# A two-layer decoder trunk on one core: retention steps, x's forms and three sets of weight sums put at other places

## The chip, the core and the metric

The kernel runs on one core of one Trainium2 chip. The core has five engines that run side by side, each through its own list of instructions in order: TensorE (PE: matmuls, with the weight loads shown apart as PEld), VectorE (DVE), ScalarE (ACT), GpSimd (POOL, hardly used here) and SyncE (SP, whose queue issues nearly all transfers). They wait for each other by semaphores. Matmul results land in PSUM banks, from which DVE and ACT fetch them; all other tiles lie in SBUF. The metric is the time on the device in microseconds (us), lower is better.

## What is computed

Two layers of a decoder over 512 tokens of width 1024, then a final RMS norm. All in float32. Cut to one layer:

```python
h = rmsnorm(x, g_mix)
z = h @ w_in
aq, ak, av, rq, rk, rv, rg, ga, gb = jnp.split(z, SPLIT_POINTS, axis=-1)
...
ya = sliding_window_sink_attention(aq, ak, av, sinks) @ w_a
...
r = chunkwise_retention(rq, rk, rv)
r = r * lax.rsqrt(jnp.mean(r * r, axis=-1, keepdims=True) + EPS)
r = r.reshape(B, S, RET_V) * jax.nn.silu(rg.astype(jnp.float32))
yb = r.astype(x.dtype) @ w_b
mixed = jax.nn.sigmoid(ga) * ya + jax.nn.sigmoid(gb) * yb
x = x + mixed @ w_out
h2 = rmsnorm(x, g_mlp)
x = x + jnp.square(jax.nn.relu(h2 @ w_up)) @ w_down
```

Attention has 8 query heads of 64 and 2 key heads, in a window of 128. Retention has 4 heads with keys of 128 and values of 256; with no chunks it is, per head, a product of scores, decayed by distance, with the values. The feed-forward width is 4096.

## The kernel before

**Precision.** Every factor is split in two parts, `hi` (rounded to the format that PE takes) and `lo` (the rest), and each product is three matmuls: hi·hi, hi·lo, lo·hi (`products`, lines 351 to 359). So a weight unit of 128 x 1024 is loaded as `raw` by SP, turned into `hi` by an ACT copy (L311) and into `lo` by a DVE subtraction (L312). Raw, hi and lo have three buffers each: unit i+3 is loaded when the low part of unit i has been made, and split when PE has gone through unit i.

**Activations are transposed**: 128 features by 512 tokens per tile. `chunk` (L400) computes 128 columns of a product: one unit, 24 matmuls into one bank of `ps_mm` (five banks), then `evacuate`. Ahead of each half of 12 matmuls it calls `advance(rate)`.

**Background work.** Attention and retention are Python generators in the list `background`. `advance(rate)` (L384) adds `rate` to a credit and, for each whole credit, runs the first generator up to its next `yield`, which writes that piece's instructions into the program at this place; `drain` (L396) runs what is left. Places in the program set the priorities; a planner orders each engine's list by them and by its own estimate of when the inputs are there, and hands out the buffers of the pools.

**Retention** (`retention`, L1190) does two heads: for each, scores for two blocks and then for the other two (`Head.scores`, with a decay table `dm` in a single buffer), then the two halves of the outputs (`Head.outputs`), the norm (`Head.norm`; the last head's by `inverse_rms`, L499, with a matmul with ones at L503 and a reciprocal at L505), and `finish`: two multiplications per half (L1184, L1185) and a split (L364, L365). At its end `sum_input` (L657) makes the forms of the pair's results. Its yields:

```python
for head in two:
    for js in ((0, 1), (2, 3)):
        head.scores(js)
        yield
...
while 4 * pair + 3 not in rg:
    yield
```

**Forms.** Several products are computed in a scheme with fewer multiplications (seven block products in place of eight): the moving factor comes as sums of blocks (`sum_input`: four DVE operations L667 to L671 and two splits of 128 x 1024) and the weights as sums of blocks. `narrow_pair` (L692) does this for w_b and w_out, `wide_pair` for w_up, and in the second layer `all_values` (L1033) for retention's values. Its seven `multiply` calls take two units and 24 matmuls each; between them ACT and DVE copy, add and split the banks: `eu` and `bu` are copies of 128 x 512 pairs. For it the second layer loads x once more from DRAM (`spill`), scales it (L1030) and makes forms of it: `raw_forms` (L1024), called for blocks 0 and 2.

**Weight sums made ahead.** For nine pairs of units of the second layer the sums of weight blocks are made in advance and parked in DRAM: `load_ahead` (L630) loads two units of 512 KB into two `big` tiles, `sum_ahead` (L634) makes four sums on DVE, behind the latest low part, and stores four parts (L266 to L271); `ahead` is both. The lists `PARKED` (w_b 0 and 2, w_out 6, w_up 4 and 6) and `AHEAD_VALUES` (four for the values) say which, `to_load` in which order. The first layer makes its own five sets (`PARKED`) during its mixing stage; its feed-forward makes the second layer's nine: the first three (w_out 6, w_up 4, w_up 6) at the w_down steps of the first quarter (`q == 0`), six in the last quarter.

**Order in the second layer** (`layer_body`): q, k, v of attention; attention in the background of gate_a's chunks, `qk(0)` and four rg chunks (their results in two `big` tiles `z`); then `raw_forms` 0, `qk(1)` (two chunks, retention's rk and rq of head 1), `raw_forms` 2; the product with w_a; `all_values`; then `qk(2)`, `qk(3)`, rg 4 to 7 and eight gate_b chunks (`put_aside`, L966 and L967, stored to `aside`) at 1.25 steps a half chunk, with both retention pairs in the background; `drain`; the products with w_b (L1352 on), which read retention's results and their forms; w_out; the feed-forward. The `big` pool has seven tiles of 128 x 1024, the pool of small ones (`temp`, 128 x 512) six, `ps_aux` three banks.

Of the kernel before, what the change touches and what calls it, by code (L numbers as in the profile page):

```python
# [13 lines left out]
AF = mybir.ActivationFunctionType  # L14
# [119 lines left out]
def decoder(ctx, tc, xT, x_first, w_in, w_a, w_b, w_out, w_up, w_down, tables, decay, band, triangles, g_last, out):  # L134
# [504 lines left out]
    def ahead():  # L639
        sum_ahead()  # L640
        load_ahead()

    def layer_body(layer):
# [389 lines left out]
        def all_values(form):  # L1033

            a, (e, b) = [bank(ps_aux, "rv") for _ in range(2)], [[bank(p, "rv") for p in (q, ps_mm)] for q in (ps_aux, ps_mm)]
            eu, bu = big("eu"), big("bu")

            def keep_values(pair, n, src):
                hi, lo = slots.one(), slots.one()
                split(view(hi), view(lo), src, rcol[:, n : n + 1])  # L1040
                rv[pair, n] = (hi, lo)

            def multiply(two, moving, start):
                for u in range(2):
                    hi, lo = unit("value", layer)
                    for i in range(2):
                        k, cols = 2 * u + i, slice(i * T, (i + 1) * T)
                        for j, ps in enumerate(two):
                            m = moving[k][:, :, j * P : (j + 1) * P]
                            pair = ((m[:, 0, :], m[:, 1, :]), (hi[:, cols], lo[:, cols]))  # L1050
                            products(ps, [pair], start and k == 0, k == 3, not start)

            def add_up(pair, two, kept):
                for j in range(2):
                    nc.vector.tensor_tensor(kept[:, j, :], two[j], kept[:, j, :], ALU.add)
                    keep_values(pair, 2 + j, kept[:, j, :])

            multiply(a, block(0, 0), True)
            for j in range(2):
                nc.scalar.activation(b[j], a[j], AF.Copy)  # L1060
            multiply(e, form(0), True)
            for j in range(2):
                nc.scalar.activation(eu[:, j, :], e[j], AF.Copy)
            multiply(b, form(1), False)
            for j in range(2):
                nc.scalar.activation(bu[:, j, :], b[j], AF.Copy)
            multiply(a, block(1, 0), False)
            for j in range(2):
                keep_values(0, j, a[j])
            multiply(b, form(2), False)  # L1070
            add_up(1, b, eu)
            multiply(e, block(1, 1), False)
            add_up(0, e, bu)
            multiply(b, form(3), False)
            for j in range(2):
                keep_values(1, j, b[j])

        rg, rg_next, rg_tiles = {}, {}, {}

# [144 lines left out]
        qk(0, PACE)  # L1224
        for i in range(4):
            chunk("w_in", layer, xs, put_rg(i), PACE)
        load_ahead()
        load_ahead()
        drain()
        rstd_columns()  # L1230
        with tc.issue_after(last_exp[0]):
# [5 lines left out]
        if last_layer:  # L1237
            homes_v = [forms_home() for _ in range(4)]
            by_form_v = [h[1] for h in homes_v]
            raw_forms(by_form_v, 0)  # L1240
            qk(1)
            raw_forms(by_form_v, 2)
        else:
            qk(1, between=ahead)
            values(0, ahead)
# [3 lines left out]
        for u in range(4):  # L1249
            hi, lo = unit("w_a", layer)  # L1250
            for j in range(2):
                c = 2 * u + j
                ps = bank(ps_mm, "mm")
                pairs = []
                for k in range(4):
                    cols = slice(k * 256 + j * P, k * 256 + (j + 1) * P)
                    pairs.append(((hi[:, cols], lo[:, cols]), aT[k]))
                products(ps, pairs, True, True)
                nc.vector.tensor_tensor(mixed[c], mixed[c], ps, ALU.mult)
            if u != 2:  # L1260
                ahead()
        for t in a_t:
            slots.give(*t[1])

        if last_layer:
            all_values(form_of(by_form_v))
            for t, _ in homes_v:
                slots.give(*t[1])
            background.append(retention(0))
            qk(2, 1.25)  # L1270
            qk(3, 1.25)
        else:
            background.append(retention(0))
            qk(2)
            qk(3)
            values(1)
            drain()
        background.append(retention(1))
        for i in range(4, 8):
            chunk("w_in", layer, xs, put_rg(i), 1.25)  # L1280
        gates, gate_tiles, fresh = [], [], []

        def put_aside(c):
# [7 lines left out]
            return put  # L1291

        for c in range(KD):
            chunk("w_in", layer, xs, put_aside(c), 1.25)
        drain()
        old_input()

# [250 lines left out]

        turning = []
        if not last_layer:  # L1550
            to_load.extend((layer + 1, *at) for at in (*PARKED[2:], *PARKED[:2], *AHEAD_VALUES))
        for what, q, i in mlp_sequence():
            if what == "first":
                late = group("w_up", layer, xs, [put_up] * 4, first_hooks())
            elif what == "pair":
                pair(q, i, late)
                if (q, i) == (3, 3):
                    old_input()
                    for t, _ in homes_x:
                        slots.give(*t[1])  # L1560
            elif what == "down":
                if (layer, q, i) == (DEPTH - 1, 2, 2):
                    turning = turns(0)
                two_chunks("w_down", layer, up[q], [put_down(2 * i), put_down(2 * i + 1)], turning)
                if i == 3:
                    slots.give(*up_slots[q])
                if not last_layer and q == 0:
                    sum_ahead()
                    if i < 3:
                        load_ahead()  # L1570
            elif layer == DEPTH - 1:
# [202 lines left out]
```

## Time and profile before

| | us |
|---|---|
| median of 3 runs | 1480.32 (1478.83 to 1480.66) |
| the profiled execution, its time | 1481.1 |
| the profiled execution, its span | 1479.2 |
| first layer: up to | about 765 |
| second layer: value product | about 898 to 938 |
| second layer: qk(2) to the last gate_b chunk | about 938 to 1046 |
| second layer: feed-forward from | about 1130 |

The profile is one execution on the chip. Its page shows busy time and count per engine; the other views cut the same record by stretches of time, by waits, by tiles, or list it in order of time. A line such as `L311 ACT ACTIVATE hi<-raw` is: line of the kernel, engine, operation, tile written and tiles read. In a timeline row the first two numbers are start and duration in us, the last entry in brackets the idle time of that engine before it and what ended it. An idle engine costs time only where PE ends up waiting for it. Matmuls are pipelined: a busy PE says that work is there, and the granted clock (1.00 is full) how fast it goes.

### The profile page before, as it was taken

The numbers are of one execution on the slowest core, as the hardware profiler recorded it, in microseconds if no ns is written. First come the engines' busy times: TensorE is split into PE (matmuls) and PEld (weight loads), VectorE is DVE, ScalarE is ACT, GpSimd is POOL, SyncE is SP. The second block draws the span as 40 slices with busy tenths as digits, with TensorE's granted clock in tenths as the row PEclk, the third lists the DMA queues.
The fourth block names the chain that finished last, engine by engine and source line by source line (L and its number), as shares of the span: only waits on it lengthen the run. The fifth ranks groups of instructions, "written<-read, shape, count | busy, mean of one in ns | idle before, by whom it ended". The sixth has DMA issues, their size and how long they took to land.

```text
span 1479.2 us, 20294 instructions
## 1 busy us (share of the span) xinstructions
PE 1461.5 (99%) x7410; PEld 1244.8 (84%) x7410; DVE 1187.6 (80%) x1950; ACT 831.4 (56%) x1330; POOL 3.7 (0%) x14
## 2 busy tenths in 40 slices
PE   9999999999999999999999999999799999999998
PEld 7888888888988888888888878888789888888887
DVE  7998778678988887776898886867889877877774
ACT  6657356654784445544455675666546844445444
POOL 0000000000000000000000000000000000000000
PEclk9999999999999999999999999999899999999999
DMA  6423843256445443334973235423464433332363
GB/s 226 134 88 108 275 161 105 93 185 210 124 128 188 164 136 100 100 100 163 324 254 113 86 129 160 139 86 124 133 212 122 130 101 99 114 115 91 111 199 112
DMA packets 80547, 212.29 MB, mean 144 GB/s; under 512 B 9512, under 2 KB 9664, under 8 KB 80448
## 3 DMA queue, kind: packets, MB, share of 16 engines
q1 hardware_dynamic: 80160, 210.48, 44.6%
q8 instruction: 58, 0.95, 0.3%
q10 hardware_dynamic: 288, 0.52, 0.1%
q14 instruction: 41, 0.34, 0.1%
HBM read 183.16 MB, written 25.18 MB: 141 GB/s over the span
## 4 chain that ended last, share of the span: by engine, by line
PE 95%; DVE 2%; ACT 1%; issue 1%; DMA 0%; POOLq 0%; DVEq 0%; ACTq 0%
PE mm L357 23%; PE mm L358 23%; PE mm L359 23%; PE mm L1454 11%; PE mm L1455 5%; PE rv L358 2%; PE rv L357 2%; PE rv L359 2%; PE score L905 1%; PE r L357 1%; PE r L359 1%; PE r L358 1%; ACT hi L311 1%; DVE lo L312 0%; PE pT L860 0%
## 5 line engine op out<-in xcount | busy, mean ns | idle before, releaser
L357 PE MATMUL mm<-r,hi 128*128 128x512 f32 (+1 forms) x1568 | 571.1, 368 | 7.9 <-ACT r L364 6.9
L358 PE MATMUL mm<-r,hi 128*128 128x512 f32 (+1 forms) x1568 | 574.3, 368 | 2.6 <-DVE r L365 2.6
L359 PE MATMUL mm<-r,lo 128*128 128x512 f32 (+1 forms) x1568 | 564.6, 368 | 0.2
L311 ACT ACTIVATE hi<-raw 128x1024 fp32r<-128x1024 f32 (+1 forms) x340 | 340.2, 1003 | 368.2 <-PE mm L358 184.9
L312 DVE TENSOR_TENSOR lo<-raw,hi 128x512 fp32r<-128x512 f32 (+1 forms) x341 | 392.2, 1153 | 102.3 <-ACT hi L311 100.6
L357 PEld LDWEIGHTS mm<-r,hi 128*128 128x128 f32 x1568 | 295.2, 189 | 56.1 <-ACT r L364 7.7
L358 PEld LDWEIGHTS mm<-r,hi 128*128 128x128 f32 x1568 | 295.5, 189 | 48.9 <-DVE r L365 3.2
L359 PEld LDWEIGHTS mm<-r,lo 128*128 128x128 f32 x1568 | 294.9, 189 | 48.8 <-DVE lo L312 1.4
L1454 PE MATMUL mm<-r,hi 128*128 128x512 f32 x728 | 252.6, 391 | 0.5 <-ACT mm L1481 0.5
L1455 PE MATMUL mm<-r,lo 128*128 128x256 f32 x728 | 200.3, 277 | 0.2 <-DVE lo L312 0.2
L1454 PEld LDWEIGHTS mm<-r,hi 128*128 128x128 f32 x728 | 136.5, 188 | 30.1 <-ACT mm L1481 1.3
L1455 PEld LDWEIGHTS mm<-r,lo 128*128 128x128 f32 x728 | 136.7, 188 | 3.9 <-DVE lo L312 1.3
L1527 ACT ACTIVATE z<-z 128x512 f32<-128x512 f32 x56 | 32.4, 623 | 49.9 <-DVE z L1507 49.7
L1534 DVE TENSOR_TENSOR x<-x,mm 128x512 f32<-128x512 f32 x56 | 37.7, 686 | 21.0 <-PE mm L359 21.0
L364 ACT ACTIVATE r<-z 128x512 fp32r<-128x512 f32 x64 | 38.3, 621 | 21.7 <-DVE z L1185 21.6
L358 PE MATMUL rv<-lo,r 128*128 128x512 f32 x120 | 46.8, 390 | 0.0
L359 PE MATMUL rv<-hi,r 128*128 128x512 f32 x120 | 46.7, 390 | 0.0
L365 DVE TENSOR_TENSOR r<-z,r 128x512 fp32r<-128x512 f32 x64 | 42.8, 686 | 4.3 <-ACT r L364 3.9
L357 PE MATMUL rv<-hi,r 128*128 128x512 f32 x120 | 45.1, 390 | 0.0
L932 ACT ACTIVATE sm<-sm,st 128x256 f32<-128x256 f32 (+1 forms) x64 | 30.1, 472 | 18.7 <-DVE st L920 18.6
L1507 DVE SCALAR_TENSOR_TENSOR z<-z,rstd 128x512 f32<-128x512 f32 x52 | 35.8, 688 | 0.6
L365 DVE TENSOR_TENSOR r<-sums,r 128x1024 fp32r<-128x1024 f32 x28 | 33.8, 1219 | 0.0
(284 smaller groups left out, 1707.4 us busy)
## 6 DMA issues: line engine op xcount, KB each, us to landing
raw<-w_in_in SPq DMA_DIRECT2D x87, 512.0 KB, 3.6
raw<-w_down_in SPq DMA_DIRECT2D x64, 512.0 KB, 3.6
raw<-w_up_in SPq DMA_DIRECT2D x32, 512.0 KB, 3.8
raw<-w_up_in SPq DMA_DIRECT2D x60, 256.0 KB, 2.9
raw<-w_a_in SPq DMA_DIRECT2D x8, 512.0 KB, 3.7
ahead<-w_b_in SPq DMA_DIRECT2D x8, 512.0 KB, 6.3
park_w_b<-ahead SPq DMA_DIRECT2D x16, 256.0 KB, 5.3
ahead<-w_up_in SPq DMA_DIRECT2D x8, 512.0 KB, 4.1
```

The lines of the kernel that those rows point to most:

```text
L311: nc.scalar.activation(hi[:, at], raw[:, at], AF.Copy)
L312: last_low[:] = [nc.vector.tensor_tensor(lo[:, at], raw[:, at], f32(hi[:, at]), ALU.subtract).ins]
L357: nc.tensor.matmul(ps, ah, bh, start=start and i == 0, stop=False, **more)
L358: nc.tensor.matmul(ps, ah, bl, start=False, stop=False, **more)
L359: nc.tensor.matmul(ps, al, bh, start=False, stop=stop and i == n - 1, **more)
L364: nc.scalar.activation(hi, src, AF.Copy)
L365: nc.vector.tensor_tensor(lo, src, f32(hi), ALU.subtract)
L1454: nc.tensor.matmul(both, hi[:, c], m, start=start and k == 0, stop=False, **more)
L1455: nc.tensor.matmul(ps[:, :H], lo[:, c], m[:, 0, :], start=False, stop=k == 3 and start, **more)
L1507: nc.vector.scalar_tensor_tensor(z[:, :, at], z[:, :, at], 0.0, factor, ALU.max, ALU.mult)
L1527: nc.scalar.activation(z[:, i, :], z[:, i, :], AF.Square)
L1534: nc.vector.tensor_tensor(x[:, c, :], x[:, c, :], ps, ALU.add)
```

## The change

Four things, nearly all of them in the second layer:

- From `qk(2)` to the last gate_b chunk the rate is 1.7 steps a half chunk in place of 1.25.
- `raw_forms` 0 is called between the two chunks of `qk(1)`, not ahead of them; `raw_forms` 2 after the first unit of w_a, not ahead of w_a.
- The list of sets to load begins with w_b and the values; w_out 6, w_up 4 and w_up 6 come last. The first quarter of the first layer's feed-forward makes no sets, the last quarter six, and the last three are made by four `ahead()` calls in `all_values`.
- `eu` and `bu` are four small tiles in place of two big ones.

```diff
-            eu, bu = big("eu"), big("bu")
+            eu, bu = [[temp("kept") for _ in range(2)] for _ in range(2)]
...
                 for j in range(2):
-                    nc.vector.tensor_tensor(kept[:, j, :], two[j], kept[:, j, :], ALU.add)
-                    keep_values(pair, 2 + j, kept[:, j, :])
+                    nc.vector.tensor_tensor(kept[j], two[j], kept[j], ALU.add)
+                    keep_values(pair, 2 + j, kept[j])
...
                 nc.scalar.activation(b[j], a[j], AF.Copy)
+            ahead()
             multiply(e, form(0), True)
...
             multiply(b, form(1), False)
...
+            ahead()
             multiply(a, block(1, 0), False)
...
             add_up(1, b, eu)
+            ahead()
             multiply(e, block(1, 1), False)
...
                 keep_values(1, j, b[j])
+            ahead()
...
-        load_ahead()
-        load_ahead()
+        if not last_layer:
+            load_ahead()
+            load_ahead()
...
-            raw_forms(by_form_v, 0)
-            qk(1)
-            raw_forms(by_form_v, 2)
+            qk(1, between=lambda: raw_forms(by_form_v, 0))
...
-            if u != 2:
-                ahead()
+            if not last_layer:
+                if u != 2:
+                    ahead()
+            elif u == 0:
+                raw_forms(by_form_v, 2)
...
-            qk(2, 1.25)
-            qk(3, 1.25)
+            qk(2, 1.7)
+            qk(3, 1.7)
...
-            chunk("w_in", layer, xs, put_rg(i), 1.25)
+            chunk("w_in", layer, xs, put_rg(i), 1.7 if last_layer else 1.25)
...
-            chunk("w_in", layer, xs, put_aside(c), 1.25)
+            chunk("w_in", layer, xs, put_aside(c), 1.7 if last_layer else 1.25)
...
-            to_load.extend((layer + 1, *at) for at in (*PARKED[2:], *PARKED[:2], *AHEAD_VALUES))
+            to_load.extend((layer + 1, *at) for at in (*PARKED[:2], *AHEAD_VALUES, *PARKED[2:]))
...
-                if not last_layer and q == 0:
-                    sum_ahead()
-                    if i < 3:
-                        load_ahead()
...
-                    ahead()
+                    (ahead if c < KD - 1 else sum_ahead)()
```

More of the change, by code (lines that the diff above doesn't have):

```diff
@@ L1060, in all_values @@
                 nc.scalar.activation(b[j], a[j], AF.Copy)
+            ahead()
             multiply(e, form(0), True)
             for j in range(2):
-                nc.scalar.activation(eu[:, j, :], e[j], AF.Copy)
+                nc.scalar.activation(eu[j], e[j], AF.Copy)
             multiply(b, form(1), False)
             for j in range(2):
-                nc.scalar.activation(bu[:, j, :], b[j], AF.Copy)
+                nc.scalar.activation(bu[j], b[j], AF.Copy)
+            ahead()
             multiply(a, block(1, 0), False)
```

## The prediction, made before the changed kernel ran

> **What bounds the kernel now.** I read the page first, for the busiest engine.
>
> ```profile
> span 1479.2 us, 20294 instructions
> PE 1461.5 (99%) x7410; PEld 1244.8 (84%) x7410; DVE 1187.6 (80%) x1950; ACT 831.4 (56%) x1330; POOL 3.7 (0%) x14
> ```
>
> TensorE (PE) is the bound almost everywhere, and the change adds and removes no matmul. So all that can be won are PE's idle stretches, 17.7 us in all by these rows, and what a low clock costs it; all that can be lost are new ones. The profiled execution took 1481.1 us (span 1479.2 and 1.9 around it), the median of the three shown runs is 1480.32: I sum against 1481.1 and subtract 0.8 at the end. A measurement of this kernel can tell a change of about 0.2%, 3 us.
>
> Next I cut the span into windows. Columns: stretch, its length, busy time (count) of PE, PEld, DVE, ACT, POOL, granted clock, DMA share, GB/s. The one large hole is in the second layer, where the gate chunks end and the product with w_b begins:
>
> ```profile
> 1045.00:1050.00 5.00, 4.88 (x36) 4.42 (x34) 3.10 (x2) 2.00 (x3) 0.00 (x0) 1.00 0.50 132
> 1050.00:1055.00 5.00, 0.38 (x1) 0.19 (x1) 4.93 (x7) 1.56 (x3) 0.00 (x0) 0.96 0.30 87
> 1055.00:1060.00 5.00, 2.23 (x7) 1.64 (x7) 5.00 (x9) 4.73 (x7) 0.00 (x0) 0.50 0.50 178
> 1060.00:1065.00 5.00, 4.37 (x20) 4.31 (x21) 3.36 (x5) 2.76 (x5) 0.00 (x0) 0.52 0.44 155
> 1065.00:1070.00 5.00, 5.00 (x45) 5.00 (x44) 3.51 (x6) 1.84 (x3) 0.00 (x0) 1.00 0.77 242
> ```
>
> PE idles 0.1 + 4.6 + 2.8 + 0.6 = 8.1 us, and then runs at half clock: its 7 + 20 matmuls took 2.23 + 4.37 = 6.6 us, at the last row's 45 in 5 us they take 3.0. Together **11.7 us**. The timeline shows what it waits for, PE first, DVE behind:
>
> ```profile
> 1045.83 0.39 PE L503 MATMUL ssq<-sh,ones 128*128 128x512 f32 x1
> ...
> 1054.03 0.38 PE L357 MATMUL mm<-r,hi 128*128 128x256 f32 x1 [4.15 <-ACT r L364]
> ...
> 1060.63 0.58 PE L358 MATMUL mm<-r,hi 128*128 128x256 f32 x1 [0.94 <-DVE r L365]
> ```
>
> ```profile
> 1048.04 3.35 DVE L505 RECIPROCAL inv<-inv 128x512 f32<-128x512 f32 x1
> 1051.42 1.29 DVE L1184 TENSOR_TENSOR z<-z,inv 128x512 f32<-128x512 f32 x2
> ...
> 1055.76 2.48 DVE L966 TENSOR_TENSOR gb<-mm,rstd 128x512 f32<-128x512 f32 x4
> ...
> 1060.82 1.22 DVE L365 TENSOR_TENSOR r<-sums,r 128x1024 fp32r<-128x1024 f32 x1
> ```
>
> That is the tail of the last retention head: its norm (L503, L505) starts when the gate chunks are already done, and its outputs and forms (L1184, L365 r<-sums) end at 1062.0, 16.2 us behind PE's last gate chunk (1045.8). The first layer has the same tail, in time:
>
> ```profile
> 315.83 1.22 DVE L365 TENSOR_TENSOR r<-sums,r 128x1024 fp32r<-128x1024 f32 x1
> ```
>
> ```profile
> 318.85 0.51 PE L359 MATMUL mm<-r,lo 128*128 128x512 f32 x2
> ```
>
> It ends at 317.1, 2 us ahead of the last gate chunk (319.1).
>
> **Retention at 1.7.** No instruction is added; the same ones are written out earlier. By its `yield`s a pair takes 17 steps (scores 4, outputs 1, 1 and 2, the first norm 1, the last output 3, the second norm 2, the two ends 2, the forms 1), and the first pair's 17th shares a step with the second's first: 33 for both. From qk(2) to the last gate chunk there are 4 + 4 + 8 + 16 = 32 half chunks, 12 matmuls of 0.227 us each, 2.7 us. At 1.25 step 33 falls in half chunk 27, at 1.7 in half chunk 20 (rg 7, for which the second pair waits, is written by half chunk 16, before the pair asks). Written ahead of the end of the chunks: 5 half chunks or 13.6 us now, 12 or 32.6 us then. Now the chain ends 16.2 us behind the end, so it lags its place in the code by 29.8 us; in the first layer step 17 falls in half chunk 14 of 24, 10 or 27 us ahead, and ends 2 us ahead: a lag of 25. With a lag of 25 to 30 the chain would end 3 to 8 us **before** PE needs it, and the whole 11.7 us goes. If the lag grows by 12 us, the chain ends 9 us late instead of 16.2, and about 7 of the 11.7 go. I take -11.7 (ends -11.7 and 0). The denser steps can make PE wait for a bank of ps_aux (three of them): no row of this stage shows such a wait at 1.25, so 0 to 3, I take +0.5.
>
> **x's forms a step later.** PE's other hole in this layer is at the end of attention (PE, ACT, DVE rows):
>
> ```profile
> 868.87 0.50 PE L357 MATMUL mm<-r,hi 128*128 128x512 f32 x1 [1.02 <-DVE z L1087]
> ...
> 875.94 1.19 PE L357 MATMUL mm<-r,hi 128*128 128x512 f32 x4 [1.34 <-ACT r L364]
> ```
>
> ```profile
> 871.78 1.32 ACT L1030 ACTIVATE xr<-xr,x 128x512 f32<-128x512 f32 x2
> ...
> 874.05 1.32 ACT L1030 ACTIVATE xr<-xr,x 128x512 f32<-128x512 f32 x2
> 875.27 0.61 ACT L364 ACTIVATE r<-whole 128x512 fp32r<-128x512 f32 x1
> ```
>
> ```profile
> 868.13 2.48 DVE L1087 TENSOR_TENSOR z<-mm,rstd 128x512 f32<-128x512 f32 x4
> ```
>
> The forms' scalings (L1030, 2.6 us on ACT) stand in front of attention's last split, for which PE waits 1.34 us; a chunk later they are behind it. The 1.02 us is four rg chunks evacuated at once; they too compete with the forms' four big tiles. I take -2.0 (ends -2.4, and +3 below). Cover: each raw_forms moves by one step, two loads on SP, 4 scalings, 4 sums, 2 splits on ACT and DVE each:
>
> ```profile
> L671 DVE TENSOR_TENSOR sums<-xr,sums x2: 683/684/684, 878.6 to 891.7; 128x512 f32<-128x512 f32 x2
> L1063 ACT ACTIVATE eu<-rv x2: 598/599/600, 906.2 to 908.9; 128x512 f32<-128x512 f32 x2
> ```
>
> The second one's last sum ran at 891.7. One unit of w_a (24 matmuls, 5.4 us) later it ends near 898; the product with form 0, copied out from 906.2 on, reads it in its second half, after 903. Five us are left; if DVE eats them, that product waits 3 us, the bound above.
>
> **Three sets out of the first layer's feed-forward.** The second layer has the same stage without them:
>
> ```profile
> 430.00:530.00 100.00, 99.28 (x515) 83.89 (x514) 85.12 (x136) 53.02 (x81) 0.00 (x0) 1.00 0.54 179
> 1168.00:1268.00 100.00, 100.00 (x529) 85.60 (x528) 81.24 (x128) 54.56 (x85) 0.00 (x0) 1.00 0.38 119
> ```
>
> 0.7 us of idle, and 14 matmuls fewer (2.6 us at 100/529), though the windows needn't begin at the same matmul. I take -1.5 (ends -2.6, -0.7). The other six sets keep their places in w_down's last quarter: they were numbers 4 to 9 and are now 1 to 6, w_b and the values in the same order. The calls that the second layer loses (two loads after rg, one step after each w_a unit) found an empty list before: nothing.
>
> **The same three sets in the value product.** A set is two loads, four sums and four stores:
>
> ```profile
> ahead<-w_up_in SPq DMA_DIRECT2D x8, 512.0 KB, 4.1
> park_w_b<-ahead SPq DMA_DIRECT2D x16, 256.0 KB, 5.3
> ```
>
> ```profile
> L271 SPq DMA_DIRECT2D park_w_out<-ahead x4: 320/323/326, 475.0 to 478.6; - x4
> L266 DVE TENSOR_TENSOR ahead<-ahead x3: 684/685/687, 474.3 to 515.4; 128x512 f32<-128x512 f32 x3
> ```
>
> 2.1 MB and 2.7 us of DVE (4 x 0.685) each; a set's stores hold SP for 3.9 us (475.0 to 478.9). The value product (about 905 to 938) against the densest stage of the trace:
>
> ```profile
> 720.00:760.00 40.00, 40.00 (x179) 33.10 (x178) 35.10 (x46) 18.16 (x25) 0.00 (x0) 1.00 1.00 361
> 905.00:938.00 33.00, 33.00 (x150) 27.42 (x149) 24.19 (x30) 19.79 (x27) 0.00 (x0) 1.00 0.59 186
> ```
>
> DVE has 8.8 us free and gets 8.2. The transfers go from 186 to 186 + 6.3 MB / 33 us = 377 GB/s, while 361 is what a full DMA share moves: 1.4 us too much. So loads will be late; how late may they be? In this stage and in the dense one, issue to landing (min/median/max):
>
> ```profile
> DMA to landing us min/median/max: 3.3/3.8/4.4
> ```
>
> ```profile
> DMA to landing us min/median/max: 6.3/6.5/6.7
> ```
>
> ```profile
> 910.51 1.23 DVE L312 TENSOR_TENSOR lo<-raw,hi 128x1024 fp32r<-128x1024 f32 x1 [0.62 <-ACT hi L311]
> ...
> 918.18 1.23 DVE L312 TENSOR_TENSOR lo<-raw,hi 128x1024 fp32r<-128x1024 f32 x1 [1.01 <-ACT hi L311]
> ```
>
> ```profile
> 917.09 1.06 ACT L311 ACTIVATE hi<-raw 128x1024 fp32r<-128x1024 f32 x1 [1.17 <-PE rv L359]
> ```
>
> The buffer freed at 911.7 is loaded by about 915.6 and split at 917.1: 1.5 us of slack. The split waits for PE to free a buffer, so two units (5.4 us) remain before PE needs it at 922.5; its low part is done at 919.4: 3.1 more, 4.6 in all. A landing of 6.5 takes 2.7 of them and four sums in DVE's queue ahead of a low part another 2.7: 0.8 us of waiting per set, 2.4. The highest bound is a load that also sits in SP's queue for half a set's stores (2 us): 2.8 per set, 8. Lower bound 0, as the dense stage shows no idle PE. I take +2.0. The copies eu and bu keep their shape (L1063); four of the six small buffers now hold them.
>
> **Sum:** 1481.1 - 11.7 + 0.5 - 2.0 - 1.5 + 2.0 = 1468.4, less 0.8: **1467.6 us**.
>
> **Rivals.** *Half the gain.* Retention's first scores ran early, inside the value product:
>
> ```profile
> L1137 DVE TENSOR_TENSOR s<-ret,dm x6: 415/548/692, 926.0 to 948.1; 128x512 f32<-128x512 f32 x2, 128x384 f32<-128x384 f32 x2, 128x256 f32<-128x256 f32 x2
> ```
>
> With the sums on DVE and the small buffers full they go back behind 938: 12 us more lag. 7 of the 11.7 are won and the value product costs 5: 1481.1 - 7 - 2 - 1.5 + 5 - 0.8 = 1474.8. Against it: the lag so far was fed by the end of the chain, not its start. *No change.* The second pair's chain is bound by its own waits and by a DVE that the sums fill, and ends no earlier: 1481.1 - 3.5 + 2 - 0.8 = 1478.8. Against it: both layers end by where the code puts them, within 5 us. *Slower.* The value product starves: the sums wait for their loads at the head of DVE's queue, low parts and stores behind them, raw loads behind the stores on SP. A load at 6.7, all of the stores' 3.9 and the sums' 2.7 make 2.9 + 3.9 + 2.7 - 4.6 = 4.9 per set; if each set also waits for its own loads, 4.1 more (the page's landing, above), 27 for three, and half clock adds 3.6 per 8.1 idle, 12. 1481.1 - 15.2 + 39 - 0.8 = 1504 at the worst, 1485 at half of it; it decides from 5 us per set on. For it: this stage uses a unit in 2.7 us, the dense one in 5.4. Against: 4.6 us of slack.
>
> The Trainium skill, page "TensorE: Matmul & The Clock Gate", section "Part 1: The HAM clock gate", ties half clock to an idle window of about 3.4 us. The trace agrees (4.15 idle, then 0.50). By that rule stalls shorter than 3.4 us cost no clock, and the slower case would be about 1492 at its worst, an estimate.
>
> **Numbers.** Forecast (1463 to 1472) 0.60, half the gain 0.20, no change 0.08, slower 0.12. Best case: all ends low, 1481.1 - 11.7 - 2.4 - 2.6 - 0.8 = 1463.6. The range 1463 to 1478 leaves out the slower case and most of no change. Faster 0.80, same 0.08, slower 0.12.
>
> **What would show it.** Right: no PE gap and full clock at the first w_b product, L505 about 19 us earlier against the last gate chunk; no 1.34 us wait before w_a; landings near 6.5 us in the value product with PE idle there for under 3 us. Wrong: L503 still behind the last gate chunk, or PE waiting for L312 or L311 in the value product.

## The result

The changed kernel is slower: 1494.97 us (1493.30 to 1495.96, four runs) against 1480.24 (1478.83 to 1480.66), a ratio of 1.010 with a 95% interval of 1.0083 to 1.0118. The profiled execution took 1494.64 us. The top of its page:

```profile
span 1492.7 us, 20296 instructions
...
PE 1467.8 (98%) x7410; PEld 1248.0 (84%) x7410; DVE 1188.8 (80%) x1950; ACT 828.5 (56%) x1328; POOL 3.7 (0%) x14
```

The number of matmuls is the same, and so is the work of DVE (1187.6 before). The span grew by 13.5 us. The stretches of the changed kernel, columns as in the prediction, show where:

```profile
430.00:530.00 100.00, 100.00 (x519) 85.22 (x518) 80.88 (x126) 53.02 (x81) 0.00 (x0) 1.00 0.37 119
905.00:938.00 33.00, 33.00 (x149) 27.42 (x148) 26.46 (x33) 19.32 (x24) 0.00 (x0) 1.00 0.83 271
...
970.00:985.00 15.00, 12.57 (x59) 10.25 (x57) 8.84 (x15) 8.43 (x15) 0.00 (x0) 0.99 0.32 88
985.00:1000.00 15.00, 11.56 (x37) 9.11 (x38) 11.10 (x16) 6.44 (x13) 0.00 (x0) 0.73 0.23 72
1000.00:1015.00 15.00, 12.29 (x39) 8.97 (x38) 11.99 (x21) 8.60 (x13) 0.00 (x0) 0.73 0.05 18
1015.00:1030.00 15.00, 14.49 (x73) 12.27 (x72) 8.71 (x18) 6.03 (x11) 0.00 (x0) 0.99 0.39 122
```

The same four stretches of the kernel before:

```profile
970.00:985.00 15.00, 15.00 (x68) 12.42 (x67) 10.55 (x17) 9.89 (x16) 0.00 (x0) 1.00 0.28 82
985.00:1000.00 15.00, 15.00 (x71) 12.61 (x70) 10.15 (x16) 7.10 (x13) 0.00 (x0) 1.00 0.30 95
1000.00:1015.00 15.00, 15.00 (x73) 12.63 (x73) 14.41 (x26) 10.02 (x17) 0.00 (x0) 1.00 0.38 119
1015.00:1030.00 15.00, 15.00 (x74) 12.75 (x73) 9.67 (x16) 11.93 (x17) 0.00 (x0) 1.00 0.44 142
```

The first layer's feed-forward runs without a stop now (x519 against x515 before), and the value product never stops PE. But between 970 and 1030, where PE had been busy without a break, it gets through 59 + 37 + 39 + 73 = 208 matmuls in place of 286: 9.1 us idle and two stretches at a clock of 0.73. At 286 in 60 us the 78 missing ones are 16.4 us, an estimate. The old hole behind the gate chunks is still there:

```profile
1063.14 0.58 PE L357 MATMUL mm<-r,hi 128*128 128x256 f32 x1 [4.15 <-ACT r L364]
1064.89 0.79 PE L357 MATMUL mm<-r,hi 128*128 128x256 f32 x2 [1.17 <-ACT r L364]
```

What PE waits for in the new hole stands in the timeline of the changed kernel, PE first, then DVE (all line numbers from `all_values` on are 4 higher: L1137 is L1141, L1184 is L1188, L1087 is L1091):

```profile
986.25 0.80 PE L357 MATMUL mm<-r,hi 128*128 128x512 f32 x1 [3.68 <-DVE rot L740]
...
998.63 0.79 PE L357 MATMUL mm<-r,hi 128*128 128x512 f32 x1 [1.32 <-DVE rot L740]
...
1008.84 0.79 PE L358 MATMUL ret<-r 128*128 128x512 f32 x1 [1.88 <-DVE r L365]
...
1011.25 0.79 PE L357 MATMUL mm<-r,hi 128*128 128x512 f32 x1 [0.55 <-DVE z L1091]
```

```profile
982.51 1.29 DVE L1188 TENSOR_TENSOR z<-z,inv 128x512 f32<-128x512 f32 x2 [2.64 <-DMA inv<-row]
...
985.52 0.68 DVE L740 TENSOR_TENSOR rot<-mm,tab 128x512 f32<-128x512 f32 x1
...
996.67 0.95 DVE L480 RECIPROCAL own<-own 128x128 f32<-128x128 f32 x1
997.89 0.69 DVE L740 TENSOR_TENSOR rot<-mm,tab 128x512 f32<-128x512 f32 x1 [0.27 <-ACT rot L737]
...
1003.67 1.29 DVE L1188 TENSOR_TENSOR z<-z,inv 128x512 f32<-128x512 f32 x2 [2.96 <-DMA inv<-row]
```

L740 is the rotation of qk's result; it is the last reader of a chunk's bank of `ps_mm`. A new chunk can't start before a bank is free, and there are five. L740 stands in DVE's queue behind retention's instructions, here behind L1188, which waits 2.64 us for a row. How long each chunk's result lay in its bank, from the end of the chunk's last matmul to the start of the operation that frees the bank (L740, for rg L1087, for a gate L966), is worked out from the trace, chunk by chunk in program order (rk and rq of qk(2) and qk(3), then rg 4 to 7, then the first four gates), in us, good to about 1 us:

```
before (1.25)         2  3  2 12    4  5 18 11   19 14  7  0
changed (1.7)        16 22 33 34   41 34 48 37   26 13 40 29
rate alone, 1.7 (e2)  3  7 14 16   26 21 32 26   21 14 39 29
before at 1.0 (e14)   2  4  5  2    0  1  0  0    4  3  5  0
before at 2.5 (e15)   7 18 23 22   40 35 35 30   54 29 22 17
```

A chunk takes PE some 6 us with the retention's matmuls in between, so a result can lie for some 25 us while the other four banks are filled; the rate alone is at that edge, the changed kernel beyond it. The Trainium skill has a sentence for the picture, page "Perfetto Trace Analysis", section "Identifying Performance Opportunities": gaps that recur on the engine that should be saturated can mean that there is no room for the next tile. The rows agree as to what PE waits for; the runs below show under which conditions the room is missing.

Retention itself, by the rows of its first score multiplications and of its multiplications with inv, before and after:

```profile
L1137 DVE TENSOR_TENSOR s<-ret,dm x12: 415/548/692, 926.0 to 1009.5; 128x512 f32<-128x512 f32 x4, 128x384 f32<-128x384 f32 x4, 128x256 f32<-128x256 f32 x4
...
L1184 DVE TENSOR_TENSOR z<-z,inv x8: 683/688/693, 976.5 to 1052.0; 128x512 f32<-128x512 f32 x8
```

```profile
L1141 DVE TENSOR_TENSOR s<-ret,dm x12: 409/548/694, 936.8 to 1022.0; 128x512 f32<-128x512 f32 x4, 128x384 f32<-128x384 f32 x4, 128x256 f32<-128x256 f32 x4
...
L1188 DVE TENSOR_TENSOR z<-z,inv x8: 684/688/694, 982.5 to 1061.1; 128x512 f32<-128x512 f32 x8
```

It starts 10.8 us later (936.8 against 926.0) and ends 9.1 us later. The span follows: from that last multiplication to the end it is 1479.2 - 1052.0 = 427.2 us before and 1492.7 - 1061.1 = 431.6 after. The 4.4 us more are the last gate chunk, which found no free bank and runs behind the chain (one chunk is 24 x 0.227 = 5.4 us of PE). 9.1 + 4.4 = 13.5. Counted on PE instead it is much the same: the hole's 16.4, less the 3.0 us by which this execution reaches the end of attention earlier.

### The profile page after: what moved, and what is told of

Its sections match the earlier page's. It is cut to its first block, busy times and chain, and to the rows that moved or that the text cites. A ratio compares the mean times of both kernels' runs of the same rounds, so it can differ in the third digit from the quotient of the medians.

```text
span 1492.7 us, 20296 instructions
## 1 busy us (share of the span) xinstructions
PE 1467.8 (98%) x7410; PEld 1248.0 (84%) x7410; DVE 1188.8 (80%) x1950; ACT 828.5 (56%) x1328; POOL 3.7 (0%) x14
## 4 chain that ended last, share of the span: by engine, by line
PE 94%; DVE 2%; ACT 2%; DMA 1%; issue 1%; POOLq 0%; SPq 0%; DVEq 0%; ACTq 0%
PE mm L357 22%; PE mm L359 22%; PE mm L358 22%; PE mm L1460 11%; PE mm L1461 6%; PE rv L357 2%; PE rv L359 2%; PE rv L358 2%; PE score L905 1%; DVE lo L312 1%; PE r L357 1%; PE r L359 0%; PE r L358 0%; DMA inv<-row 0%; PE pT L860 0%
```

## The experiments

In all tables "first score" and "last inv" are the first and the last start of these two rows, the time is the median, and the ratio is to the kernel before timed beside it, with its 95% interval. The two starts come from one profiled execution each. Ten kernels that are the same up to the end of attention reach it up to 2.2 us apart, so a difference of 1 or 2 us between two starts says little.

### Which part is it

e1 sets all three rates of the changed kernel back to 1.25:

```diff
-            qk(2, 1.7)
-            qk(3, 1.7)
+            qk(2, 1.25)
+            qk(3, 1.25)
...
-  put_rg(i), 1.7 if last_layer else 1.25   and   put_aside(c), 1.7 if last_layer else 1.25
+  put_rg(i), 1.25                          and   put_aside(c), 1.25
```

> The changed kernel with 1.25 steps a half chunk everywhere again; the forms and the three sets stay where the change put them. Theory rate (the denser retention steps are written ahead of the evacuations of qk(2) and qk(3), so these come late, the banks of mm stay full and PE idles between 980 and 1035): about 1478 us, 2 below before, because the feed-forward's 3 us stay won and the hole between 980 and 1035 is gone; the rot gaps on L740 are not there. Theory sets (the last set's sums push retention's first scores 11 us back, and the crowd behind them makes the hole): 1490 to 1496, the hole stays.

e2 makes the opposite edit in the kernel before. e3 is e1 with the two `raw_forms` calls put back to their old places. e12 is the changed kernel with them put back:

```diff
-            qk(1, between=lambda: raw_forms(by_form_v, 0))
+            raw_forms(by_form_v, 0)
+            qk(1)
+            raw_forms(by_form_v, 2)
...
-            elif u == 0:
-                raw_forms(by_form_v, 2)
```

> The kernel before with 1.7 steps a half chunk in the three places, nothing else changed. Theory rate: 1492 to 1498, with PE gaps that end on the rotation's evacuation (L736, L740) between 970 and 1030, and little won at the gate chunks' end. Theory sets: 1468 to 1475, as the prediction had it: the hole at 1050 to 1065 goes and none comes in its place.

> The kernel before with the three sets moved into the value product (and eu, bu in small tiles) alone, rate 1.25, forms in their old place. Theory rate: 1476 to 1480 (3 us won in the first layer's feed-forward, 0 to 2 lost behind the value product). Theory sets: 1488 to 1495, the hole between 980 and 1035 without any rate change.

> The change without its move of x's forms: rate 1.7 and the three sets. With 1.25 the move of the forms was worth -0.6 us (1483.3 against 1483.9). If it has no part in the hole: 1493 to 1497. If the forms' later place is what crowds the value product and qk at 1.7: 1482 to 1486.

| | rate | sets | forms | us | ratio | first score | last inv |
|---|---|---|---|---|---|---|---|
| before | 1.25 | | | 1480.24 | | 926.0 | 1052.0 |
| e2 | 1.7 | | | 1482.08 | 1.0008 (0.9999 to 1.0017) | 924.9 | 1048.4 |
| e3 | 1.25 | moved | | 1483.90 | 1.0019 (1.0009 to 1.0028) | 936.7 | 1055.0 |
| e1 | 1.25 | moved | moved | 1483.31 | 1.0023 (1.0013 to 1.0032) | 935.9 | 1054.4 |
| e12 | 1.7 | moved | | 1493.77 | 1.0084 (1.0067 to 1.0101) | 937.4 | 1060.7 |
| changed | 1.7 | moved | moved | 1494.97 | 1.010 (1.0083 to 1.0118) | 936.8 | 1061.1 |

Both theories fall as written: neither the rate nor the sets make the hole alone. The rate costs 1.3 us (1482.08 against 1480.82 for the kernel before beside it, an interval that just includes nothing; the two profiled executions have the same span, 1479.2), the sets with the forms 2.5, together 3.8; the whole change costs 14.7. Some 11 us are in the **pair** of them. The forms have no part that these runs can tell (e1 against e3, changed against e12).

### Where the rate does it

e4 is the kernel before with 1.7 for rg and gates only; e5 is the changed kernel with 1.25 in `qk(2)` and `qk(3)`; e16 has 0.8 there and 1.25 from rg on:

```diff
-            qk(2, 1.7)
-            qk(3, 1.7)
+            qk(2, 1.25)      (e16: 0.8, and 1.25 for rg and gates)
+            qk(3, 1.25)
```

> The kernel before with 1.25 steps in qk(2) and qk(3) and 1.7 only from the rg chunks on. Theory rate: the crowding is one of qk's evacuations, so there is no hole before 1000, and the last retention head ends some 5 half chunks (13 us) earlier: 1470 to 1476. If it is the retention chain itself that DVE and ACT can't run faster beside PE's chunks (a lag that grows as the steps get denser), the end is where it was and the time 1478 to 1486.

> The whole change, but with 1.25 steps in qk(2) and qk(3); 1.7 from the rg chunks on. Theory banks: in the changed kernel the chunks' results of qk(2) and qk(3) wait 16 to 34 us in their banks, because 1.7 puts the retention steps ahead of them on DVE and the late start adds its 11 us; when all five banks of mm are taken PE stops. With 1.25 in qk the wait falls to 11 to 21 us, as with the sets alone, no chunk waits for a bank before 1010: 1480 to 1484, and no PE gap over 1 us between 970 and 1010. Theory start (the late first scores alone make the hole, whatever the rate in qk): 1490 or more.

> The forms and the three sets moved as in the change, 0.8 steps in qk(2) and qk(3), 1.25 from there on. Theory own pace: the evacuations of qk come within 10 us again and the chain is not fed too late: its last L1188 at 1046 to 1050, so 1476 to 1480. If the sets' cost is the late start of the chain itself: 1482 to 1486, as with 1.25.

| | us | ratio | first score | last inv |
|---|---|---|---|---|
| e4 | 1478.90 | 0.9992 (0.9983 to 1.0002) | 926.1 | 1047.1 |
| e5 | 1483.51 | 1.0021 (1.0011 to 1.0031) | 936.7 | 1049.8 |
| e16 | 1484.98 | 1.0029 (1.0017 to 1.0040) | 936.7 | 1056.1 |

The 11 us hang on the rate in the four chunks of `qk(2)` and `qk(3)`: without it (e5) the first rg results are fetched as soon as they are done, and one stop of 3.79 us is left. What the sets cost at a low rate stays (e16): it is not cured by earlier evacuations, and it is what remains of the late start. e4 missed its range of 1470 to 1476. Its chain ends 4.9 us earlier, but the last gate chunk is left over, as in the changed kernel, and takes that back.

### What pushes the scores back

e6 is e2 with `eu` and `bu` in small tiles and no sets; e7 is the changed kernel with them in big tiles; e17 moves two sets, and the third is made where it was:

```diff
-            eu, bu = [[temp("kept") for _ in range(2)] for _ in range(2)]
+            eu, bu = big("eu"), big("bu")                      (e7; e6 the other way round)
...
-  (*PARKED[:2], *AHEAD_VALUES, *PARKED[2:])
+  (PARKED[2], *PARKED[:2], *AHEAD_VALUES, *PARKED[3:])         (e17)
...
+                if not last_layer and q == 0 and i in (1, 2):
+                    (load_ahead if i == 1 else sum_ahead)()
```

> The kernel before with 1.7 everywhere in the stage and eu, bu as four small tiles, but with no sets moved. Tells what pushes retention's first scores back. Theory small pool (the four copies take four of six small tiles, so that the tile s of a score block finds none): first scores near 936, and with 1.7 the bank waits of the changed kernel, 1488 to 1496. Theory sums (the sets' sums stand ahead of the scores on DVE): first scores near 926 and 1480 to 1484, as with the rate alone.

> The whole change, but with eu and bu as two big tiles again. Theory small pool: first scores near 926, 1480 to 1485 (the hole shrinks to the 2 to 3 us of the rate alone). Theory sums: first scores near 936 or later, since the sets now also have two big tiles less, 1493 to 1500.

> The whole change with 1.7 steps, but only two of the three sets in the value product; the third is made in the first layer's feed-forward, where it was. Theory late start: the sums end some 10 us earlier, the first scores run at 926 to 930, the chain ends 5 to 10 us earlier than in the changed kernel (1060.5), 1483 to 1488. If transfers and tiles decide, two thirds of the cost stay: 1490 to 1493.

| | us | ratio | first score | last inv |
|---|---|---|---|---|
| e6 | 1482.40 | 1.0016 (1.0006 to 1.0025) | 925.4 | 1049.1 |
| e7 | 1495.22 | 1.0106 (1.0089 to 1.0123) | 941.4 | 1062.1 |
| e17 | 1485.35 | 1.0032 (1.0021 to 1.0043) | 926.0 | 1049.8 |

The small tiles are not it (e6 starts at 925.4, e7 even later than the changed kernel). The third set is: with two, the scores start at 926.0 again, and 9.6 of the 14.7 us are gone. So at 1.7 the hole needs the **late start and the dense steps**; at 2.5 the dense steps make one alone (e15, below). Whether it is the third set's sums on DVE, its two tiles or its loads that put the scores behind was not separated.

### What holds the bank

The chain of waits of the changed kernel passes twice through the norm's transfers; the first time:

```profile
976.91 1.60 DMA row<-own
...
978.53 3.96 DMA inv<-row
...
982.51 1.29 DVE z L1188 x2
...
985.52 0.69 DVE rot L740
```

e8 takes one bank of `ps_mm` away from e2. e9, e10 and e11 take the transfers away, in the changed kernel, in the kernel before and in e2. e13 gives L740 its place ahead of L1188 in the changed kernel by an edge on DVE:

```diff
+            held = bank(ps_mm, "mm")                                      (e8)
+            nc.vector.memset(held[:, :P], 0.0)
...
+            nc.vector.tensor_copy(temp("held")[:, :P], held[:, :P])       (e8, behind the gates)
...
-  (inverse_rms if self.h == 3 else inverse_rms_apart)(self.parts, RET_V, self.inv)
+  (inverse_rms if self.h == 3 else inverse_rms_halved if last_layer else inverse_rms_apart)(...)    (e9, e10, e11)
...
+  last_evac[0] = nc.vector.tensor_tensor(a, a if early else ps, tabs[0], ALU.mult).ins    (e13; the same in put_rg)
...
+  with tc.issue_after(last_evac[0]) if last_layer else ExitStack():
       nc.vector.tensor_tensor(z, z, self.inv, ALU.mult)
```

> The kernel before with 1.7 steps, and one of the five banks of mm taken out of use from qk(2) to the end of the gate chunks (a small memset into it, a small copy out of it behind them). Theory banks: with the rate alone all five banks are taken from the first gate chunk on and the waits stay at 1.06 us; with four, each chunk waits till a bank comes free, 10 to 20 us in all: 1488 to 1500, with PE gaps that end on L740 or L1087 between 970 and 1030. If banks don't decide (PE stops for another reason, as the retention's own banks): 1481 to 1484.

> The whole change, but in the second layer the first three heads' norms spread 1/rms over the partitions by ACT copies (as the kernel's other norm does) and not by two transfers through DRAM. In the changed kernel the chain of waits runs twice through these transfers (5.6 us from 976.9, 6.0 us from 997.65), with the multiplication L1188 that waits for them at the head of DVE's queue, the rotation's evacuation L740 behind it, and PE behind that for a bank. Theory head of the queue: without the transfers the hole between 980 and 1035 falls from 17.7 us to 8 or less, 1480 to 1487. Theory amount (DVE simply has too much to do ahead of the evacuations): the hole stays within 3 us of what it was, 1492 to 1496.

> The kernel before, rate 1.25, with the same norms without transfers. Theory chain (the time follows the end of the last head's chain: in eight kernels so far it is the start of the last L1184 plus 429.4 us where all gate chunks are done by then, 431.9 to 434.5 where one is left): the fourth head's sum of squares (L464, 1039.85) no longer stands behind the third head's L1184 (1036.9, which waits 5.6 us for its row), so the chain ends 4 to 6 us earlier: 1474 to 1477. If the end hangs on the places in the program (as the prediction took it): 1479 to 1481.

> The kernel before at 1.7, with the norms without transfers. Theory chain: the last L1184 some 5 to 9 us ahead of the 1047.8 of the rate alone, and 1474 to 1478, because one gate chunk is left over behind it (5 us). If the prediction's lag of 25 to 30 us held once the transfers are gone: the hole at the end goes altogether, 1469 to 1472.

> The whole change, with one edge added on DVE in the second layer: the multiplication with inv (L1188) is queued behind the last evacuation of qk or rg that is written so far, so L740 of qk(3) comes ahead of the first two heads' L1188 and not behind. Theory order: no PE gap over 1 us between 980 and 1000, pair 1's scores some 10 us earlier than 999, 1482 to 1488. Theory amount (the chain's own work is what PE waits for, in whatever order): 1492 to 1497.

| | us | ratio | first score | last inv |
|---|---|---|---|---|
| e8 | 1483.87 | 1.0026 (1.0015 to 1.0037) | 926.6 | 1052.6 |
| e9 | 1493.89 | 1.0086 (1.0071 to 1.0101) | 936.7 | 1060.1 |
| e10 | 1480.52 | 0.9998 (0.9989 to 1.0007) | 925.6 | 1051.7 |
| e11 | 1482.38 | 1.0011 (1.0002 to 1.0021) | 927.1 | 1049.8 |
| e13 | 1491.74 | 1.0076 (1.0061 to 1.0091) | 938.3 | 1058.3 |

Taking the transfers out is no cure: without them (e9, e10, e11) nothing moves by more than the intervals allow. e10 and e11 missed the ranges of the theory that they were made for, 1474 to 1477 and 1474 to 1478; e10 came out where the rival had it, by which the places in the program set the end, and e14 below speaks against that rival. In e9 L740 still stands behind L1188 (1002.36 behind 1000.55), which waits for the norm's reciprocal and copies in place of the row: a link of the chain of waits was replaced, not removed. The order of this one pair is a part: e13 is 3.2 us faster than the changed kernel, just under one of its ranges (1492 to 1497) and far from the other (1482 to 1488). Its stops remain, only later:

```profile
970.00:985.00 15.00, 15.00 (x69) 12.31 (x69) 9.54 (x14) 10.71 (x17) 0.00 (x0) 1.00 0.30 100
985.00:1000.00 15.00, 12.51 (x56) 9.91 (x55) 9.75 (x15) 5.25 (x10) 0.00 (x0) 1.00 0.27 90
1000.00:1015.00 15.00, 9.03 (x24) 6.48 (x25) 15.00 (x26) 9.23 (x14) 0.00 (x0) 0.66 0.17 51
```

From 1000 to 1015 DVE has not a moment free while PE idles 6.0 us: what was put off arrives at once. e8 missed its range too: it was to cost 10 to 20 us. PE stops 6.6 us before 1040 in place of 2.3, and the hole at the end of the gate chunks shrinks in return. By the medians the time is only 1.8 us above e2; in the profiled executions the last inv is 4.2 us later and the span 4.4 us longer. So a bank less costs no more than the 4.3 us that PE stops longer. How a stop of PE reaches the chain stands in the changed kernel's rows, with one more of PE:

```profile
994.24 0.39 PE L475 MATMUL ssq<-sh,ones 128*128 128x512 f32 x1
```

This matmul of retention's norm comes right after the chunk that could only begin at 986.25. The reciprocal of its result (L480, 996.67) stands ahead of the next L740 (997.89) in DVE's list, and for that L740 PE waits again (998.63). PE waits for a bank, the bank for DVE, and DVE for a matmul behind the waiting chunk.

### Is the chain faster when it is written earlier

e14 and e15 are the kernel before with 1.0 and 2.5 in all three places. e18 has 1.0 in `qk(2)` and `qk(3)`, 1.25 behind them, and the second pair's four score steps written ahead of the first pair's last steps:

```diff
+        def retention_both():
+            first, second = retention(0), retention(1)
+            for _ in range(13):
+                next(first)
+                yield
+            for _ in range(4):
+                next(second)
+                yield
+            yield from first
+            yield from second
```

> The kernel before with 1.0 in place of 1.25. Theory own pace: the chain takes its 120 to 125 us from its first score whatever the rate, the evacuations come earlier (waits under 15 us), the last L1184 stays within 3 us of 1051.4, and the time within 3 us of before: 1477 to 1483. The prediction's picture (the chain ends 25 to 30 us behind its place in the code, 33 steps then being written out only in the last half chunks): last L1184 near 1070, 1495 to 1502.

> The kernel before with 2.5. Theory own pace and banks: all steps are written by half chunk 14, the chain ends no earlier than at 1.7 (1047.8), the evacuations of qk wait for 30 us and more, PE stops for banks: 1484 to 1496. The prediction's picture: 1468 to 1471.

> The kernel before with 1.0 in qk(2) and qk(3), 1.25 behind them, and the second pair's four score steps written ahead of the first pair's last steps (its finish and forms). If the chain's order is what makes it long: second pair's first scores near 985 in place of 991, last L1184 4 to 8 us earlier, 1472 to 1477. If it is bound by the waits inside each pair: 1477 to 1481, as with 1.0 alone.

| | rate | us | ratio | first score | last inv |
|---|---|---|---|---|---|
| e14 | 1.0 | 1479.04 | 0.9989 (0.9980 to 0.9998) | 925.3 | 1052.3 |
| before | 1.25 | 1480.24 | | 926.0 | 1052.0 |
| e2 | 1.7 | 1482.08 | 1.0008 (0.9999 to 1.0017) | 924.9 | 1048.4 |
| e15 | 2.5 | 1494.86 | 1.0097 (1.0082 to 1.0113) | 925.7 | 1048.7 |
| e18 | 1.0, then 1.25 | 1479.26 | 0.9995 (0.9986 to 1.0004) | 924.9 | 1050.5 |

This is the answer to the prediction. Over a factor of 2.5 in the rate the chain takes 127.0, 126.0, 123.5 and 123.0 us from its first score, and its last inv stays between 1052.3 and 1048.4. At 1.0 the step with the last inv, the 32nd, is written in the last of the 32 half chunks, at 1.25 in the 26th, and yet the last inv starts within 0.3 us of the same time. So at these rates it is not the writing of the steps that sets the end. The length is no constant of the chain, though: where the first scores are 10.7 us late, it is 118.3 us (e3) and 113.1 us (e5). There most of the late start is made up on the way; in the changed kernel (124.3 us) it is not. What the rate does move is the fetching of the chunks, as the table of waits showed. The rows of 1.0:

```profile
L740 DVE TENSOR_TENSOR rot<-mm,tab x4: 691/692/692, 945.5 to 968.7; 128x512 f32<-128x512 f32 x4
...
L966 DVE TENSOR_TENSOR gb<-mm,rstd x8: 683/692/693, 1001.8 to 1045.5; 128x512 f32<-128x512 f32 x8
```

and of 2.5, with PE's longest stop behind them:

```profile
L740 DVE TENSOR_TENSOR rot<-mm,tab x4: 674/686/691, 951.5 to 990.8; 128x512 f32<-128x512 f32 x4
...
L966 DVE TENSOR_TENSOR gb<-mm,rstd x8: 681/684/692, 1052.4 to 1071.2; 128x512 f32<-128x512 f32 x8
```

```profile
1053.15 0.80 PE L357 MATMUL mm<-r,hi 128*128 128x512 f32 x1 [10.28 <-DVE gb L966]
```

At 1.0 all eight gates are fetched before the chain ends; at 2.5 none is, five of them fill the banks, and three chunks are left over. From the last inv to the end it is 1477.5 - 1052.3 = 425.2 us at 1.0 and 1492.3 - 1048.7 = 443.6 at 2.5; against the 427.2 of before the 16.4 more are three chunks of 5.4. At 2.5 the rate alone costs as much as the whole change.

e14 is 1.4 us under the kernel before timed beside it, with an interval that just leaves out no change (one such in eighteen runs can be chance), and 16 us under the changed kernel: the one version here that beats both, if by less than the 0.2% that the prediction set as its bound. (e4 has the same time; its interval includes no change.) e18 is no faster: the order of the second pair's scores doesn't make the chain shorter.

## Why the prediction was wrong

The forecast was 1467.6 us, in a range of 1463 to 1478; it came out at 1494.97, slower. By its steps:

- **Retention at 1.7 (-11.7).** This is the step that failed. It took the chain to end at a fixed lag of 25 to 30 us behind its place in the program, so that steps written 19 us earlier would end 19 to 24 us earlier. e14, before, e2 and e15 show that the place has next to no say: the rate alone brings the end forward by 3.6 us (1052.0 to 1048.4; 2 to 3 in e6 and e11), a leftover chunk takes this back, and the median is 1.3 us higher. That both layers gave nearly the same lag rested on two numbers at one rate; a rate of 1.0 would have tested it.
- **The denser steps (+0.5, 0 to 3).** This term failed too, and by more. The prediction put the price at `ps_aux`, retention's own banks. It was at `ps_mm`: the pieces that are written early stand ahead of the chunks' evacuations on DVE, and with the late start this made the hole of some 16.4 us. In the prediction's terms, an estimate: 0 for retention, 0 for the forms, -3.0 for the feed-forward in this execution and +16.4 for the hole make 1481.1 + 16.4 - 3.0 = 1494.5, and the profiled execution took 1494.64. The trace of before held a warning: results that lay in their banks for up to 19 us already at 1.25 (the table of waits), and the fifth gate's for 28.
- **x's forms (-2.0).** Nothing: both gaps are still there, 2.96 us earlier with all that follows the feed-forward, and of the same size (the rows below). The scalings (L1030) start 2.96 us earlier as well, at 868.82 and 871.09 against 871.78 and 874.05, so they still stand in front of that split.

```profile
865.91 0.50 PE L357 MATMUL mm<-r,hi 128*128 128x512 f32 x1 [1.02 <-DVE z L1091]
...
872.98 1.20 PE L357 MATMUL mm<-r,hi 128*128 128x512 f32 x4 [1.34 <-ACT r L364]
```

- **Three sets out of the feed-forward (-1.5).** Right. The first matmul behind the first of these gaps starts at 865.91 here and at 868.87 before, 3.0 us earlier. One execution is not enough for this: over the nine profiled kernels with all three sets moved it starts at 865.91 to 866.90, on average 866.45, over the ten with the sets in place at 867.83 to 870.03, on average 868.66. So 2.2 us were won, inside the term's 0.7 to 2.6.
- **The sets in the value product (+2.0).** The feared late loads did not come: DMA is dense (271 GB/s, share 0.83), DVE 26.5 of 33 us, and PE has no gap. What came instead is the late start: e3 loses 3.1 us net, so 5.3 beside the 2.2 won.
- **Half the gain** named the late start and its size (12 us, measured 10.8), and took it to cost 4.7 of the 11.7 us to be won. The gain was not there to be halved, and with the dense steps the late start cost more than alone.
- **No change**, held at 0.08, had the part on retention: a chain bound by its own waits that ends no earlier. For the rate alone it is borne out (e2). What spoke against it, that both layers end by where the code puts them, is what e14 and e15 refute.
- **Slower** got the sign by a mechanism that did not happen. What did happen, PE stopped by its own five banks, was in no case of the prediction.

Shown: the two factors and their product (e1, e2, e3, e12, e5, e17), that the chain's end hardly follows the rate (e14, e15), and that taking out the transfers (e9 to e11), other tiles for `eu` and `bu` (e6, e7) or the old place of the forms (e12) cures nothing. In part argued: that the banks of `ps_mm` turn the two factors into the hole; the rows show PE waiting for them, but e8 and e13, which changed the banks and the order, moved the time by 1.8 and 3.2 us only. Open: which of the chain's links set its end (taking out the transfers or changing the order of the scores moves it by less than 2 us), and why the planner puts evacuations, whose input is ready, behind retention's pieces; that its estimate of the chain is shorter than the chip's is only argued.

## What to carry to other kernels

Before writing background work earlier, find out whether it is waiting to be issued or waiting for itself: measure where it ends at two or three rates, down too. If the end stays, a higher rate only moves it ahead of other work in the in-order queues, and the price appears where that work gives buffers back; so look at how long each result lies in its PSUM bank against the number of banks, since PE showed no idle time here until they were all taken. Two edits that each cost 1 to 3 us can cost 15 together when they draw on the same slack, so costs taken one by one don't bound the sum.

## What was unexpected of the hardware

The prediction cited a rule of the Trainium skill, page "TensorE: Matmul & The Clock Gate", section "Part 1: The HAM clock gate", that half clock needs an idle window of about 3.4 us. In the changed kernel the clock fell after much shorter stops. The PE timeline from 996.69 on:

```profile
996.69 0.39 PE L357 MATMUL ret<-r 128*128 128x256 f32 x1 [0.86 <-ACT own L479]
...
998.63 0.79 PE L357 MATMUL mm<-r,hi 128*128 128x512 f32 x1 [1.32 <-DVE rot L740]
999.22 0.63 PE L358 MATMUL mm<-r,hi 128*128 128x512 f32 x1
...
1001.36 0.52 PE L357 MATMUL mm<-r,hi 128*128 128x512 f32 x1
1001.72 0.39 PE L358 MATMUL mm<-r,hi 128*128 128x512 f32 x1
```

After a stop of 0.86 us, three matmuls and a stop of 1.32, matmuls of 128x512 show 0.63 us in place of 0.39, for 2.7 us. Again from 1008.84 on (a stop of 1.88, rows above), until 1015. The 1.34 us before w_a cost no clock (872.98, four matmuls in 1.20). The measurement decides, and the prediction's estimate that stops shorter than 3.4 us are free of it does not hold.

Neither the length of the stops nor their number decides it: e13 has the same two, 0.86 and 1.32 us with three short matmuls between them, and keeps its clock.

```profile
991.81 0.39 PE L357 MATMUL ret<-r 128*128 128x256 f32 x1 [0.86 <-ACT own L479]
...
993.76 0.50 PE L357 MATMUL mm<-r,hi 128*128 128x512 f32 x1 [1.32 <-DVE rot L742]
994.09 0.40 PE L358 MATMUL mm<-r,hi 128*128 128x512 f32 x1
```

What sets them apart is where the stops fall. In each of the twenty traces the granted clock changes only at times that lie 3.41 us, or a multiple of it, apart. Cut at these times, the changed kernel and then e13 show (columns as above):

```profile
994.80:998.21 3.41, 1.65 (x9) 1.05 (x7) 2.50 (x3) 2.98 (x7) 0.00 (x0) 1.00 0.15 35
998.21:1001.62 3.41, 2.99 (x7) 2.41 (x8) 2.46 (x5) 1.35 (x3) 0.00 (x0) 0.50 0.32 128
```

```profile
989.48:992.89 3.41, 2.10 (x11) 1.42 (x9) 2.18 (x2) 3.34 (x7) 0.00 (x0) 1.00 0.11 35
992.90:996.31 3.41, 2.55 (x11) 2.12 (x12) 3.30 (x6) 0.25 (x2) 0.00 (x0) 1.00 0.43 151
```

In the changed kernel the first stop and most of the second fall into one such stretch: PE is busy for 1.65 of its 3.41 us, and the next stretch runs at half clock. In e13 the second stop is spread over two: PE is busy for 2.10 and 2.55 us of them, and the clock stays at 1.00. Over the twenty traces 37 stretches at full clock with PE busy for at most 49% were followed by one at half clock, and none with 51% or more was; one stretch, at the very end of e2 (1.55 of 3.41 us busy, from 1472.32), does not fit.
